# Gated DeltaNet's triangular blocks inverted with 32 and 64 wide tensor engine tiles, in place of 128 wide products and transposes

## The chip, the cores and the metric

The kernel runs on one core of a Trainium2 chip. The time is that of the device from start to end of one execution, in microseconds (us). The engines of a core run in parallel, each in the order of its own instructions: the tensor engine (PE, with its weight loads as PEld), VectorE (DVE), ScalarE (ACT), GpSimd (POOL), and SyncE (SP), which here only issues transfers between HBM and on-chip memory. A transfer is issued by an engine's queue and waits there, with all that is queued behind it, until what it needs is there.

## The reference

Four residual layers, each a token mixer, a cross-attention and a gated MLP; layer 2's mixer is the gated DeltaNet, which alone is touched. It works on 256 tokens, 8 query/key heads and 16 value heads, in chunks. Within a chunk it solves a unit lower triangular system:

```
    decay = jnp.exp(jnp.where(incl, gc[..., :, None] - gc[..., None, :], -jnp.inf))
    kb = k * beta[..., None]
    m = jnp.where(strict, jnp.einsum('bnhlk,bnhsk->bnhls', kb, k) * decay, 0.0)
    a_mat = m + jnp.eye(chunk, dtype=jnp.float32)
    rhs = jnp.concatenate([v * beta[..., None], kb * jnp.exp(gc)[..., None]], axis=-1)
    sol = lax.linalg.triangular_solve(a_mat, rhs, left_side=True, lower=True, unit_diagonal=True)
```

## The kernel before

Weights come from HBM as 128x1024 tiles (`raw`, four buffers, loaded by SP). ScalarE casts each to its high part `wH`, VectorE subtracts to get the low part `wL` (`prep`), and the tensor engine takes three products for each pair of parts (`mm3`, lines 168 to 170). One tile feeds 24 such products of 128x256, called weight products below. In the DeltaNet they go to the PSUM tile `gps` (48 tiles) and then to `acc` (16 tiles of the output projection).

`gdn` works on chunks of 128 tokens. A head of the loop is a query/key head with two value heads and two chunks, so it has four 128x128 triangular matrices, index `a`, kept side by side in a 128x512 tile. `head` is a generator: at each `yield cost, latency` it hands back to a scheduler of the program (`Weave`), which runs the next piece once the projections have issued that many nanoseconds of tensor engine work. So the work of several heads is woven between weight products. The compiler's scheduler then settles the order within each engine. The names in a head, in its order:

- `l2` and `grb`: norms of query and key, and the decays by row; `E` the decays.
- `gp` (line 942): the products of keys with keys and queries. VectorE makes `MT` from it, the transposed triangular matrices with their decays (line 948).
- SP stores `MT` to a scratch in HBM (`gd`, line 956) and loads its 16x16 diagonal blocks back as `blk` (line 957), 32 blocks on 32 partitions.
- GpSimd inverts these blocks by substitution in 30 instructions (`tm`, `ub`, lines 969 and 971) and stores the result to a second scratch, zeroed outside the blocks (line 973).
- SP loads that as `U` (line 987), the inverse so far, transposed.
- The solve. Four transposes give `Tm` from `U` (`tps`). Then blocks of 16 are joined to blocks of 32, and those to 64: with the part of `MT` that a level needs (`ml`, masked by `lvl`), `yps` = ml x Tm, `ups` = U x Y, Tm -= ups, and four transposes write U anew. The last level, 64 to 128, uses 64x64 products and writes U directly.
- Then the right-hand sides: `gvp`, `gsp`, `gs`, `grp`, `gop`, and at the end `gbp`. `S` is the state, copied out of `gs` by ScalarE.

All small products are float32 and run as two passes on the tensor engine, so that four products show as x8 in the rows.

Of the kernel before, what the change touches and what calls it, by code (L numbers as in the profile page):

```python
# [40 lines left out]
CM = {}  # L41
# [45 lines left out]
def tile_trunk(ctx: ExitStack, tc: tile.TileContext, io: dict, out: bass.AP, layers=range(DEPTH), parts="mxf", final=True):  # L87
    nc = tc.nc
    ACT, DVE, POOL, PE = nc.scalar, nc.vector, nc.gpsimd, nc.tensor
# [21 lines left out]
    def mx(name):  # L111
        return ps_mx.tile([P, 512], F32, tag="mx", name=name)
# [4 lines left out]
    def flat(ap):  # L117
        return ap.rearrange("p a b -> p (a b)")
# [19 lines left out]
    cm = cst.tile([P, CM["bd"]], F32, name="cm")  # L138
# [705 lines left out]
    def diag(d):  # L844
        return bass.AP(tensor=d.tensor, offset=d.offset, ap=[[16 * P + 16, 32], [P, 16], [1, 16]])

    def rows(d):
        return d[:, :P, :].rearrange("a s l -> s a l")

    def gdn_scratch():  # L850
        with phase("gz") as z:
            zt = z.tile([P, 4, P], F32, name="zt")
            POOL.memset(zt, 0.0)
            d = [[dr.tile([4, P + 1, P], F32, name=f"gd{i}{j}") for j in range(2)] for i in range(2)]
            for j in range(2):
                nc.sync.dma_start(out=rows(d[1][j]), in_=zt)
        return d

    def gdn(layer, ic, gname):
        with ExitStack() as ex:  # L860
# [4 lines left out]
            gcm = U1([P, 768], "gcm")  # L865
            nc.scalar.dma_start(out=gcm, in_=io["cm"][:, CM["lvl"]:CM["lvl"] + 768])
# [8 lines left out]
            (a, b), (c, d) = [[flat(t[:, :2]), flat(t[:, 2:])] for t in (U1([P, 4, P], "E"), U1([P, 4, P], "Y"))]  # L875
            rw, tcol = U1([P, T], "grw", F32R), U1([P, 2, 64], "gtcol")
            POOL.memset(pk, 0.0)
            with tc.high_priority(offset=EVAC):
# [8 lines left out]
                DVE.tensor_tensor_scan(out=pk[:16], data0=gcm[:16, 512:768], data1=ga, initial=0.0,  # L887
# [13 lines left out]
            lvl = gcm[:, :2 * P].rearrange("p (a b) -> p a b", a=2)  # L901
# [4 lines left out]
            def head(h, qk):  # L906
# [48 lines left out]
                d0, d1 = scr[0][h % 2], scr[1][h % 2]  # L955
# [5 lines left out]
                ml = W(f"ml{h % 2}", 1)  # L961

                def level(l):
                    DVE.tensor_tensor(out=ml, in0=MT, in1=lvl[:, l:l + 1, :].to_broadcast([P, 4, P]), op=ALU.mult)

                POOL.tensor_copy(ub.rearrange("p a b -> p (a b)"), gcm[:32, 256:512])
# [6 lines left out]
                nc.gpsimd.dma_start(out=diag(d1), in_=ub)  # L973
                kd, qd = W2("kd", 3), W2("gqd", 3)
# [19 lines left out]
                Tm = W("Tm")  # L994
                ACT.copy(flat(Tm), tps)
                yield 440, LAT[2]
                for l in range(2):
                    yp = mx("yps")
                    for a in range(4):
                        PE.matmul(yp[:, a * P:(a + 1) * P], ml[:, a, :], Tm[:, a, :], start=a == 0, stop=True,  # L1000
                                  skip_group_check=True)
                    if l == 0:
                        level(1)
                    Y = W("Y", 1)
                    ACT.copy(flat(Y), yp)
                    yield 870, LAT[3]
                    up = mx("ups")
                    for a in range(4):
                        PE.matmul(up[:, a * P:(a + 1) * P], U[:, a, :], Y[:, a, :], start=a == 0, stop=True,
                                  skip_group_check=True)  # L1010
                    DVE.tensor_tensor(out=flat(Tm), in0=flat(Tm), in1=up, op=ALU.subtract)
                    yield 870, LAT[4]
                    tps = mx("tps")
                    for a in range(4):
                        PE.transpose(tps[:, a * P:(a + 1) * P], Tm[:, a, :], ident)
                    ACT.copy(flat(U), tps)
                    yield 440, LAT[14]

                yp = mx("yps")
                for a in range(4):  # L1020
                    PE.matmul(yp[64:, a * 64:(a + 1) * 64], MT[:64, a, 64:], Tm[:64, a, :64], start=a == 0, stop=True,
                              skip_group_check=True)
                Y = W("Y", 1)
                ACT.copy(Y[64:, :, :64], yp[64:, :T].rearrange("p (a b) -> p a b", a=4))
                yield 440, LAT[3]
                up = mx("ups")
                for a in range(4):
                    PE.matmul(up[:64, a * 64:(a + 1) * 64], Y[64:, a, :64], U[64:, a, 64:], start=a == 0, stop=True,
                              skip_group_check=True)
                DVE.tensor_tensor(out=U[:64, :, 64:], in0=U[:64, :, 64:], in1=up[:64, :T].rearrange("p (a b) -> p a b", a=4),  # L1030
                                  op=ALU.subtract)
                yield 440, LAT[13]
# [309 lines left out]
```

## Time and profile before

| | us |
|---|---|
| median of 3 executions | 2039.09 |
| lowest, highest | 2039.07, 2043.4 |
| profiled execution | 2039.35 |
| its span, first to last instruction | 2037.6 |
| tensor engine busy | 1987.2 (98%) |
| VectorE busy | 1575.0 (77%) |
| ScalarE busy | 1280.4 (63%) |
| GpSimd busy | 341.6 (17%) |

Busy is the time in which at least one instruction of the engine is under way. The share is a mean over a program of many stages, and says nothing of which engine a single stage waits for. The DeltaNet mixer lies between about 985 and 1285 us.

### The profile page before, as it was taken

How to read it: one execution, taken by the hardware profiler on the slowest of the kernel's cores; microseconds unless marked ns; L12 is line 12 of the kernel's file. 1: busy time of each engine (PE TensorE's matmuls, PEld its weight loads, DVE VectorE, ACT ScalarE, POOL GpSimd, SP SyncE). 2: the span in 40 equal slices, each digit the busy share in tenths (PEclk: the TensorE clock that was granted, in tenths of full speed). 3: DMA queues.
4: the chain of work that ended last, by engine and by line, in shares of the span. 5: the costliest groups of instructions: out<-in, count | busy, mean ns of one | idle time of the engine just before them, and what ended most of it. 6: DMA issues, size and time to landing. Idle time of an engine off the chain costs nothing.

```text
span 2037.6 us, 42013 instructions
## 1 busy us (share of the span) xinstructions
PE 1987.2 (98%) x17020; PEld 1942.3 (95%) x17020; DVE 1575.0 (77%) x2417; ACT 1280.4 (63%) x1874; POOL 341.6 (17%) x468
## 2 busy tenths in 40 slices
PE   8999999999999999999999999999999999999997
PEld 8999999999999899999998899999999999999997
DVE  6899777875788778866786875878756999777875
ACT  6687666654565566555676875666545778666553
POOL 2032211000133110001064451110001133201001
PEclk9999999999999999999999999999999999999999
DMA  7655545666644546666544333457666565545663
GB/s 242 202 186 173 174 146 167 216 193 181 211 156 135 150 133 211 200 192 192 188 123 136 107 111 123 140 162 217 193 177 200 196 197 171 179 136 176 195 193 121
DMA packets 112770, 351.53 MB, mean 173 GB/s; under 512 B 15744, under 2 KB 25664, under 8 KB 112576
## 3 DMA queue, kind: packets, MB, share of 16 engines
q1 hardware_dynamic: 106176, 333.42, 52.9%
q10 hardware_dynamic: 6144, 15.17, 2.2%
q8 instruction: 133, 2.18, 0.4%
q0 software_dynamic: 256, 0.26, 0.1%
q14 instruction: 61, 0.50, 0.1%
HBM read 344.81 MB, written 4.00 MB: 171 GB/s over the span
## 4 chain that ended last, share of the span: by engine, by line
PE 78%; issue 5%; DVE 5%; ACT 4%; POOL 2%; DMA 1%; DVEq 0%; SPq 0%; POOLq 0%; ACTq 0%
PE ffps L170 8%; PE ffps L169 8%; PE ffps L168 8%; PE acc L168 6%; PE acc L169 6%; PE acc L170 6%; PE mps L168 4%; PE mps L170 3%; PE mps L169 3%; DVE wL L161 2%; PE qps L170 2%; PE qps L168 2%; PE qps L169 2%; PE kvps L168 1%; PE kvps L170 1%
## 5 line engine op out<-in xcount | busy, mean ns | idle before, releaser
L161 DVE TENSOR_TENSOR wL<-raw,wH 128x1024 fp32r<-128x1024 f32 (+2 forms) x639 | 786.3, 1232 | 326.8 <-ACT wH L160 324.3
L160 ACT CAST wH<-raw 128x1024 fp32r<-128x1024 f32 (+2 forms) x639 | 658.9, 1032 | 535.6 <-PE ffps L169 160.8
L168 PE MATMUL ffps<-hH,wH 128*128 128x256 f32 x1376 | 380.6, 277 | 0.0
L169 PE MATMUL ffps<-hL,wH 128*128 128x256 f32 x1376 | 379.8, 276 | 0.0
L170 PE MATMUL ffps<-hH,wL 128*128 128x256 f32 x1376 | 379.2, 276 | 0.0
L168 PE MATMUL acc<-aH,wH 128*128 128x256 f32 x1232 | 344.5, 280 | 0.0
L170 PE MATMUL acc<-aH,wL 128*128 128x256 f32 x1232 | 341.4, 277 | 0.6 <-DVE wL L161 0.6
L169 PE MATMUL acc<-aL,wH 128*128 128x256 f32 x1232 | 341.0, 277 | 0.0
L169 PEld LDWEIGHTS ffps<-hL,wH 128*128 128x128 f32 x1376 | 258.3, 188 | 0.1
L168 PEld LDWEIGHTS ffps<-hH,wH 128*128 128x128 f32 x1376 | 258.3, 188 | 0.1
L170 PEld LDWEIGHTS ffps<-hH,wL 128*128 128x128 f32 x1376 | 258.0, 188 | 0.0
L168 PEld LDWEIGHTS acc<-aH,wH 128*128 128x128 f32 x1232 | 231.5, 188 | 1.3 <-issue 0.7
L170 PEld LDWEIGHTS acc<-aH,wL 128*128 128x128 f32 x1232 | 231.3, 188 | 1.1 <-DVE wL L161 1.0
L169 PEld LDWEIGHTS acc<-aL,wH 128*128 128x128 f32 x1232 | 231.6, 188 | 0.6
L168 PE MATMUL mps<-hH,wH 128*128 128x256 f32 x768 | 218.0, 284 | 0.0
L169 PE MATMUL mps<-hL,wH 128*128 128x256 f32 x768 | 213.8, 278 | 0.0
L170 PE MATMUL mps<-hH,wL 128*128 128x256 f32 x768 | 213.0, 277 | 0.0
L212 POOL TENSOR_TENSOR ns<-nsq 128x256 f32<-128x256 f32 x13 | 10.7, 821 | 856.7 <-ACT nsq L209 856.7
L168 PEld LDWEIGHTS mps<-hH,wH 128*128 128x128 f32 x768 | 144.3, 188 | 2.9 <-issue 2.4
L169 PEld LDWEIGHTS mps<-hL,wH 128*128 128x128 f32 x768 | 144.4, 188 | 0.7
L170 PEld LDWEIGHTS mps<-hH,wL 128*128 128x128 f32 x768 | 144.4, 188 | 0.3
L170 PE MATMUL gps<-hH,wL 128*128 128x256 f32 x448 | 127.6, 285 | 0.6 <-DVE wL L161 0.6
(410 smaller groups left out, 4670.1 us busy)
## 6 DMA issues: line engine op xcount, KB each, us to landing
raw<-f_up SPq DMA_DIRECT2D x176, 512.0 KB, 4.1
raw<-m_in SPq DMA_DIRECT2D x96, 512.0 KB, 3.6
raw<-f_down SPq DMA_DIRECT2D x80, 512.0 KB, 4.2
raw<-xa_kv SPq DMA_DIRECT2D x60, 512.0 KB, 4.3
raw<-g_in SPq DMA_DIRECT2D x48, 512.0 KB, 4.1
raw<-m_out SPq DMA_DIRECT2D x32, 512.0 KB, 3.6
raw<-xa_q SPq DMA_DIRECT2D x32, 512.0 KB, 3.6
raw<-xa_o SPq DMA_DIRECT2D x32, 512.0 KB, 3.6
```

The costliest lines, as they stand in the source:

```text
L160: ACT.copy(H[:, c], raw[:, c])
L161: DVE.tensor_tensor(out=L[:, c], in0=raw[:, c], in1=f32(H[:, c]), op=ALU.subtract)
L168: PE.matmul(dst, aH, bH, start=start, stop=False, skip_group_check=True)
L169: PE.matmul(dst, aH, bL, start=False, stop=False, skip_group_check=True)
L170: PE.matmul(dst, aL, bH, start=False, stop=stop, skip_group_check=True)
L212: self.eng.tensor_tensor(out=self.sum, in0=sq[:, :T], in1=sq[:, T:], op=ALU.add)
```

## The change

The inverse is kept in both forms from the start. GpSimd writes its blocks also transposed (`ut`) to a third scratch, and SP loads from it `Tm`, now only the 64 columns that are used, in two halves. Each level is done on the diagonal tiles alone: level 16 with products on 32x32 tiles (for `up` with 16 columns), level 32 likewise, level 64 with 64x64 tiles. Both `U` and `Tm` are updated from products, with no transposes and no masked copy of `MT`; a per-partition factor `low` (made once from `lvl`) clears the part that level 16 must not take. Since all products of the solve go through one helper, they carry its one line (1000) in the changed kernel. The constants are loaded in two pieces, and two of the softplus scratch tiles take other places.

```diff
-            d = [[dr.tile([4, P + 1, P], F32, name=f"gd{i}{j}") for j in range(2)] for i in range(2)]
+            d = [[dr.tile([4, P + 1, P], F32, name=f"gd{i}{j}") for j in range(2)] for i in range(3)]
             for j in range(2):
-                nc.sync.dma_start(out=rows(d[1][j]), in_=zt)
+                for i in (1, 2):
+                    nc.sync.dma_start(out=rows(d[i][j]), in_=zt)
...
+            DVE.tensor_reduce(out=low, in_=lvl, axis=AX.X, op=ALU.max)
+            DVE.tensor_scalar(out=low, in0=low, scalar1=-1.0, scalar2=1.0, op0=ALU.mult, op1=ALU.add)
...
                 nc.gpsimd.dma_start(out=diag(d1), in_=ub)
+                POOL.tensor_copy(ut, ub.rearrange("p a b -> p b a"))
+                nc.gpsimd.dma_start(out=diag(d2), in_=ut)
...
                 nc.sync.dma_start(out=U, in_=rows(d1))
-                level(0)
+
+                Tm = wk.tile([P, 4, 64], F32, tag="Tm", name="Tm", bufs=2)
+                for b in (0, 64):
+                    nc.sync.dma_start(out=Tm[b:b + 64], in_=d2[:, b:b + 64, b:b + 64].rearrange("a s l -> s a l"))
                 yield 0, LAT[1]
-
-                tps = mx("tps")
+                Q = [slice(32 * i, 32 * i + 32) for i in range(4)]
+                quad = lambda ps, o, w: ps[:, o:o + 4 * w].rearrange("p (a b) -> p a b", a=4)
+
+                def block(d, lhsT, rhs, first):
+                    PE.matmul(d, lhsT, rhs, start=first, stop=True, skip_group_check=True)
+
+                ps = mx("yps")
+                yp = quad(ps, 0, 16)
                 for a in range(4):
-                    PE.transpose(tps[:, a * P:(a + 1) * P], U[:, a, :], ident)
...
+                    for i, q in enumerate(Q):
+                        block(yp[q, a], MT[q, a, q], Tm[q, a, 32 * (i % 2):32 * (i % 2) + 16], a == 0)
+                Y = wk.tile([P, 4, 16], F32, tag="Y0", name="Y0", bufs=1)
+                ACT.activation(out=Y, in_=yp, func=AF.Copy, scale=low)
+                yield 300, 1200
+                ps = mx("ups")
+                tp, up = quad(ps, 0, 16), quad(ps, 64, 16)
                 for a in range(4):
...
+                    for q in Q[:3]:
+                        block(tp[q, a], U[q, a, q], Y[q, a], a == 0)
                 for a in range(4):
...
+                    for i, q in enumerate(Q):
+                        block(up[32 * i:32 * i + 16, a], Y[q, a], U[q, a, 32 * i + 16:32 * i + 32], a == 0 and i == 3)
+                for i in (0, 2, 1):
+                    d = Tm[Q[i], :, 32 * (i % 2):32 * (i % 2) + 16]
+                    DVE.tensor_tensor(out=d, in0=d, in1=tp[Q[i]], op=ALU.subtract)
+                for i in (1, 3, 0, 2):
+                    ACT.activation(out=U[32 * i:32 * i + 16, :, 32 * i + 16:32 * i + 32], in_=up[32 * i:32 * i + 16], func=AF.Copy,
+                                   scale=-1.0)
+                yield 600, 1800
+
+                ps = mx("yps")
+                yp = quad(ps, 0, 32)
+                for a in range(4):
+                    for b in (0, 2):
+                        block(yp[Q[b + 1], a], MT[Q[b], a, Q[b + 1]], Tm[Q[b], a, :32], a == 0)
...
+                yield 300, 1200
+                ps = mx("ups")
+                tp, up = quad(ps, 0, 32), quad(ps, P, 32)
+                for a in range(4):
+                    block(tp[Q[1], a], U[Q[1], a, Q[1]], Y[Q[1], a], a == 0)
+                    for b in (0, 2):
+                        block(up[Q[b], a], Y[Q[b + 1], a], U[Q[b + 1], a, Q[b + 1]], a == 0)
...
+                yield 400, 1500
+
+                ps = mx("yps")
+                yp = quad(ps, 0, 64)
+                for a in range(4):
+                    block(yp[64:, a], MT[:64, a, 64:], Tm[:64, a, :], a == 0)
...
```

The change also alters the order on the engines. On SP, from head 0's `U` on (the scratches are numbered; `gd_12451` and `gd_12452` hold U's blocks, `gd_12453` the transposed ones), before:

```order
L987 DMA U<-gd_12451 128x4x128
L159 DMA raw<-g_in 128x1024
L956 DMA gd_12450<-MT 128x4x128
L957 DMA blk<-gd_12450 32x16x16
L159 DMA raw<-g_in 128x1024 x3
L987 DMA U<-gd_12452 128x4x128
L159 DMA raw<-g_in 128x1024
```

and in the changed kernel:

```order
L990 DMA U<-gd_12451 128x4x128
L994 DMA Tm<-gd_12453 64x4x64
L962 DMA gd_12450<-MT 128x4x128
L994 DMA Tm<-gd_12453 64x4x64
L963 DMA blk<-gd_12450 32x16x16
L159 DMA raw<-g_in 128x1024 x4
L962 DMA gd_12449<-MT 128x4x128
L990 DMA U<-gd_12452 128x4x128
```

Head 1's MT and block loads stand between the halves of Tm and the next weights, and no weight is loaded between U and MT any more. On GpSimd, at the end of head 0's block, before:

```order
L969 TENSOR_TENSOR tm<-ub,blk 32x15
L971 TENSOR_TENSOR ub<-ub,tm 32x15
L973 DMA gd_12451<-ub 32x16x16
L966 COPY ub<-gcm 32x256
L960 TENSOR_TENSOR gatt<-gatt,cm 128x512
```

and in the changed kernel:

```order
L970 TENSOR_TENSOR tm<-ub,blk 32x15
L972 TENSOR_TENSOR ub<-ub,tm 32x15
L974 DMA gd_12451<-ub 32x16x16
L975 COPY ut<-ub 32x256
L976 DMA gd_12453<-ut 32x16x16
L967 COPY ub<-gcm 32x256
L966 TENSOR_TENSOR gatt<-gatt,cm 128x512
```

The copy `ut` and its store have come in behind U's store, ahead of the next head's work. On the tensor engine, where head 7's solve starts (weight products to `acc`), in the changed kernel:

```order
L1118 MATMUL gbp<-ident,on 128x128 x4
L1000 MATMUL yps<-Tm,MT 32x32 x8
L1000 MATMUL yps<-Tm,MT 32x16 x16
L1000 MATMUL ups<-Y_15884,U 32x32
L1000 MATMUL ups<-U,Y_15884 32x32
L168 MATMUL acc_15846<-aH,wH 128x256
L169 MATMUL acc_15846<-aL,wH 128x256
L170 MATMUL acc_15846<-aH,wL 128x256
L1000 MATMUL ups<-Y_15904,U 32x16 x12
L1000 MATMUL ups<-U,Y_15904 16x16 x16
```

Where before a group was four transposes or four 128-wide products, it is now 8 to 28 small ones. Here head 7's first group (32x16, x16) stands 94 weight products behind its `gp`; before, its first transposes stood 193 behind.

## Rows read from the trace of the kernel before

**Rows 1.** The page, busy time of the tensor engine and its weight loads, with share of the span and instructions.

```profile
PE 1987.2 (98%) x17020; PEld 1942.3 (95%) x17020; DVE 1575.0 (77%) x2417; ACT 1280.4 (63%) x1874; POOL 341.6 (17%) x468
```

**Rows 2.** Busy time of each engine from 1015.1 to 1266 us: length, then busy us (instructions) of PE, PEld, DVE, ACT and POOL, granted tensor engine clock, DMA share, GB/s.

```profile
1015.10:1266.00 250.90, 240.58 (x1935) 225.46 (x1936) 183.23 (x357) 182.34 (x276) 112.78 (x262) 0.99 0.38 120
```

**Rows 3.** Timeline of the tensor engine from 1015.1 to 1266 us: start us, us until the last of them ends, what; in brackets the idle time before it and what ended it. The heads: `gp` at 1015.13 is head 0, 1101.31 head 3, 1133.31 head 4; `tps` at 1127.35 is head 3, 1161.33 head 4, 1244.40 head 7; `grp` is head 0; `gbp` head 6.

```profile
1015.13 0.70 PE L942 MATMUL gp<-kq 128*128 128x256 f32 x2 [0.64 <-DVE kq L919]
...
1073.11 0.80 PE L1064 MATMUL grp<-S,kd 128*128 128x128 f32 x2 [3.21 <-ACT S L1059]
...
1101.31 1.03 PE L942 MATMUL gp<-kq 128*128 128x256 f32 x4
...
1127.35 0.60 PE L993 MATMUL tps<-ident,U 128*128 128x128 f32 x4
...
1133.31 1.03 PE L942 MATMUL gp<-kq 128*128 128x256 f32 x4
...
1161.33 0.66 PE L993 MATMUL tps<-ident,U 128*128 128x128 f32 x4 [1.23 <-DMA U<-gd]
...
1244.40 0.60 PE L993 MATMUL tps<-ident,U 128*128 128x128 f32 x4
...
1265.95 0.60 PE L1091 MATMUL gbp<-ident,on 128*128 128x128 f32 x4
```

**Rows 4.** Waits of the SP queue between 980 and 1290 us: who waits, for what: us in total, times, longest us.

```profile
SPq L987 <- DMA gd<-ub: 86.2, 8, 16.9
```

**Rows 5.** Timeline of the SP queue: start us, us, issue. The first four are around U of head 0, then U of head 1 with the weight behind it, then U of heads 3, 6 and 7.

```profile
1041.11 0.38 SPq L987 DMA_DIRECT2D U<-gd  x1
1041.58 0.46 SPq L159 DMA_DIRECT2D raw<-g_in  x1
1042.09 0.42 SPq L956 DMA_DIRECT2D gd<-MT  x1
1047.63 0.33 SPq L957 DMA_DIRECT2D blk<-gd  x1
...
1066.36 0.38 SPq L987 DMA_DIRECT2D U<-gd  x1
1066.84 0.45 SPq L159 DMA_DIRECT2D raw<-g_in  x1
...
1123.00 0.38 SPq L987 DMA_DIRECT2D U<-gd  x1
...
1219.64 0.37 SPq L987 DMA_DIRECT2D U<-gd  x1
...
1234.78 0.38 SPq L987 DMA_DIRECT2D U<-gd  x1
```

**Rows 6.** Timeline of the tensor engine in heads 0 and 2 (columns as in rows 3). `gps` is a weight product, `tps` transposes, `yps` at 1048.74 the 128-wide products, at 1060.65 the 64-wide ones.

```profile
1044.74 0.60 PE L993 MATMUL tps<-ident,U 128*128 128x128 f32 x4
...
1045.30 0.28 PE L170 MATMUL gps<-hH,wL 128*128 128x256 f32 x1
...
1047.42 0.28 PE L170 MATMUL gps<-hH,wL 128*128 128x256 f32 x1
...
1048.74 1.06 PE L1000 MATMUL yps<-Tm,ml 128*128 128x128 f32 x8
...
1049.76 0.28 PE L169 MATMUL gps<-hL,wH 128*128 128x256 f32 x1
...
1060.12 0.60 PE L1015 MATMUL tps<-ident,Tm 128*128 128x128 f32 x4
1060.65 0.68 PE L1021 MATMUL yps<-Tm,MT 64*64 64x64 f32 x8
...
1061.48 0.28 PE L169 MATMUL gps<-hL,wH 128*128 128x256 f32 x1
```

**Rows 7.** Timeline of the tensor engine in the HGRN2 mixer of layer 1, a group with 32-column outputs between weight products.

```profile
586.97 0.28 PE L170 MATMUL ips<-wH,hL 128*128 128x256 f32 x1
587.18 0.64 PE L759 MATMUL op<-S,qd 128*32 128x128 f32 x14
...
587.97 0.28 PE L169 MATMUL ips<-wL,hH 128*128 128x256 f32 x1
```

**Rows 8.** Timeline of GpSimd in head 2: first of the block, two in between, the store, and the copy behind it; the DVE row is the cast that runs at the same time.

```profile
1074.17 0.20 POOL L969 TENSOR_TENSOR tm<-ub,blk 32x15 f32<-32x15 f32 x1 [6.14 <-DMA blk<-gd]
...
1077.42 0.29 POOL L969 TENSOR_TENSOR tm<-ub,blk 32x60 f32<-32x60 f32 x1
1077.78 1.16 POOL L971 TENSOR_TENSOR ub<-ub,tm 32x60 f32<-32x60 f32 x1
...
1086.45 0.68 POOL L973 DMA_DIRECT2D gd<-ub  x1 [0.30 <-POOL ub L971]
1088.62 0.39 POOL L966 COPY ub<-gcm 32x256 f32<-32x256 f32 x1 [1.49 <-DMA gd<-ub]
...
1077.46 1.33 DVE L161 TENSOR_TENSOR wL<-raw,wH 128x1024 fp32r<-128x1024 f32 x1 [2.27 <-ACT wH L160]
```

**Rows 9.** DMA issues: what, queue, number, size of one, median us from issue to landing.

```profile
gd<-MT SPq DMA_DIRECT2D x8, 256.0 KB, 2.5
U<-gd SPq DMA_DIRECT2D x8, 256.0 KB, 2.8
```

**Rows 10.** The instructions that write the masked copy `ml`: line, engine, operation, number: ns least/median/most, first and last start, shapes.

```profile
L964 DVE TENSOR_TENSOR ml<-MT,gcm x16: 676/686/701, 1025.5 to 1247.0; 128x512 f32<-128x512 f32 x16
```

More of the change, by code (lines that the diff above doesn't have):

```diff
@@ L864, in gdn @@
             oT = U1([P, 16, T], "goT")
-            gcm = U1([P, 768], "gcm")
-            nc.scalar.dma_start(out=gcm, in_=io["cm"][:, CM["lvl"]:CM["lvl"] + 768])
+            gcm = U1([P, 512], "gcm")
+            nc.scalar.dma_start(out=gcm, in_=io["cm"][:, CM["i16"]:CM["i16"] + 512])
+            lvl, low = U1([P, P], "glvl"), U1([P, 1], "glow")
+            nc.scalar.dma_start(out=lvl, in_=io["cm"][:, CM["lvl"]:CM["lvl"] + P])
+            DVE.tensor_reduce(out=low, in_=lvl, axis=AX.X, op=ALU.max)
+            DVE.tensor_scalar(out=low, in0=low, scalar1=-1.0, scalar2=1.0, op0=ALU.mult, op1=ALU.add)
             baps = bank("baps")
@@ L874, in gdn @@
             be = flat(be)[32:48]
-            (a, b), (c, d) = [[flat(t[:, :2]), flat(t[:, 2:])] for t in (U1([P, 4, P], "E"), U1([P, 4, P], "Y"))]
+            (a, b), (c, d) = [[t[:, 0, :], t[:, 1, :]] for t in (flat(U1([P, 4, P], "E")).rearrange("p (a b) -> p a b", a=2), U1([P, 2, T], "gsq"))]
             rw, tcol = U1([P, T], "grw", F32R), U1([P, 2, 64], "gtcol")
@@ L885, in gdn @@
                 DVE.tensor_scalar(out=ga, in0=ga, scalar1=na, scalar2=None, op0=ALU.mult)
-                DVE.tensor_tensor_scan(out=pk[:16], data0=gcm[:16, 512:768], data1=ga, initial=0.0,
+                DVE.tensor_tensor_scan(out=pk[:16], data0=gcm[:16, 256:512], data1=ga, initial=0.0,
                                        op0=ALU.mult, op1=ALU.add)
@@ L900, in gdn @@
             cols = weave.push(late(12000, columns()))
-            lvl = gcm[:, :2 * P].rearrange("p (a b) -> p a b", a=2)
             W = lambda nm, b=2: wk.tile([P, 4, P], F32, tag=nm, name=nm, bufs=b)
@@ L954, in head @@
                 tm = wk.tile([32, 16, 16], F32, tag="tm", name="tm", bufs=1)
-                d0, d1 = scr[0][h % 2], scr[1][h % 2]
+                ut = wk.tile([32, 16, 16], F32, tag="ut", name="ut", bufs=1)
+                d0, d1, d2 = [s[h % 2] for s in scr]
                 nc.sync.dma_start(out=rows(d0), in_=MT)
@@ L960, in head @@
                 POOL.tensor_tensor(out=att, in0=att, in1=tri.unsqueeze(1).to_broadcast([P, 4, P]), op=ALU.mult)
[L961 to L966, printed above, removed]
+                POOL.tensor_copy(ub.rearrange("p a b -> p (a b)"), gcm[:32, :256])
                 for j in range(15):
@@ L995, in head @@
[L995 to L1017, printed above, removed]
@@ new lines, in head @@
+                for i in (1, 3, 0, 2):
[7 more added lines that the diff above has]
+                        block(yp[Q[b + 1], a], MT[Q[b], a, Q[b + 1]], Tm[Q[b], a, :32], a == 0)
+                Y = wk.tile([P, 4, 32], F32, tag="Y1", name="Y1", bufs=1)
@@ new lines, in head @@
+                ACT.copy(Y[Q[1]], yp[Q[1]])
+                DVE.tensor_copy(Y[Q[3]], yp[Q[3]])
+                yield 300, 1200
[5 more added lines that the diff above has]
+                        block(up[Q[b], a], Y[Q[b + 1], a], U[Q[b + 1], a, Q[b + 1]], a == 0)
+                DVE.tensor_scalar(out=Tm[Q[1], :, :32], in0=tp[Q[1]], scalar1=-1.0, scalar2=None, op0=ALU.mult)
@@ new lines, in head @@
+                for b in (2, 0):
+                    ACT.activation(out=U[Q[b], :, Q[b + 1]], in_=up[Q[b]], func=AF.Copy, scale=-1.0)
+                yield 400, 1500
[3 more added lines that the diff above has]
+                    block(yp[64:, a], MT[:64, a, 64:], Tm[:64, a, :], a == 0)
+                Y = wk.tile([P, 4, 64], F32, tag="Y", name="Y", bufs=1)
+                ACT.copy(Y[64:], yp[64:])
+                yield 480, 1200
@@ L1034, in head @@
+                ps = mx("ups")
+                up = quad(ps, 0, 64)
+                for a in range(4):
+                    block(up[:64, a], Y[64:, a, :], U[64:, a, 64:], a == 0)
+                DVE.tensor_scalar(out=U[:64, :, 64:], in0=up[:64], scalar1=-1.0, scalar2=None, op0=ALU.mult)
+                yield 480, LAT[13]
                 while h not in vz or (h and h - 1 not in done):
```

13 lines of the change are left out of this document (removed).

## The prediction

> **What bounds the kernel now.** I read the page first: the tensor engine is busy 98% of the span [rows 1], so only its work or its waits can move the end. Then I asked for the stretch that the change touches, from head 0's first `gp` product (1015.13) to head 6's `gbp` (1265.95): 250.9 us, in which the tensor engine is busy 240.6 and idle 10.3 [rows 2, 3]. The rest of the span is the same in both kernels.
>
> Then I looked for what ends the idle time, and found a chain beside the tensor engine. Each head's products give MT; SP stores it and loads its 16x16 blocks back; GpSimd inverts them in 30 small instructions (`tm`, `ub`); GpSimd stores the result, and SP loads U. SP runs in order and also loads the weights, so weight loads behind a waiting U wait too: SP spends 86.2 us before the eight U loads, up to 16.9 at once [rows 4]. Two of the tensor engine's waits end with it: 1.23 us for U itself in head 4, and 3.21 us at 1073.11 in head 0 [rows 3], where, in ScalarE's order, the copy of S stands behind the cast of the weight that SP issued only at 1066.84, right behind U [rows 5]. Elsewhere the tensor engine has enough other work between a head's `gp` and its first product on U: in heads 3 and 7 that product starts without a wait [rows 3].
>
> **The tensor engine's own work.** Prices from one stretch [rows 6]: a weight product 0.118 us (18 steps from 1045.30 to 1047.42); four transposes 0.44 (1044.74 to 1045.30, less one product); four 128-wide float32 products, two passes each, 0.90 (1048.74 to 1049.76, less one); four 64-wide ones 0.80 (1060.12 to 1061.48, less the transposes and one weight product). A head's solve is now 3 x 0.44 + 4 x 0.90 + 2 x 0.80 = 6.5 us.
>
> The new solve has no transposes, 64 products on 32x32 tiles (128 passes) and the two 64-wide groups. Nothing in the trace is that small. The nearest row is the other mixer's group of 14 passes with 32-column outputs: 586.97 to 587.97 is 1.00 us, less two weight products 0.76 [rows 7]. One after the other at the 128-wide price (0.90 / 8 = 0.11 each) they would take 1.6, so passes on different column tiles do run side by side: four rounds of 0.11 explain 0.44, and the 0.33 left is the cost of changing the array's shape and back. The 64-wide group then has 0.47 for 8 passes, 0.058 each. A small pass costs at most those 0.058 (7.4 us a head, all in a row); with half the columns and two to four tiles at once it is 0.007 to 0.015. I take the latter, nearest to the row with the same tile width: 1.3 us a head. With six changes of shape (2.0) and 0.94 for the 64-wide passes a solve is 4.3 us, 2.2 less. Counting every group in both orders at these prices, the same stretch has 241.8 us of work before (the trace says 240.6 busy, so the count holds) and 17.3 us less after, five groups split by weight products included.
>
> The Trainium skill speaks against the small products: "TensorEngine Tiling (Array Packing)", section Instruction Overhead, gives each matmul some 60 cycles however few its columns, and advises against tiling a dimension that is already small. By it, estimated at the granted clock (0.99 of 2.4 GHz in this stretch [rows 2]), 128 passes would cost 3.2 us a head instead of 1.3, and the gain would be 2 us instead of 17.3. The row of 14 passes agrees that passes overlap but does not show so few columns.
>
> **What is added to the chain.** Behind U's store GpSimd now copies the transposed blocks (0.39, as its copy at 1088.62) and issues a second store (0.68, as at 1086.45) [rows 8]; SP issues U, waits for that store, and issues Tm in two loads. The first product needs Tm. Bounds: 0.5 if the stores overlap fully, 2 if copy and store each meet a VectorE cast; I take 1.1. Behind the waiting Tm loads stand the next MT store or block load and then the weights.
>
> VectorE and ScalarE lose more than they gain (two masks, two 128x512 subtractions and five 128x512 copies a head go, small operations come); they end no wait above except through casts, so this counts nothing. Two more zero stores and the split constant load at the mixer's start go out while four weights are loaded ahead; without that cover they cost the two issues, under 1 us. The scratch tiles of the softplus change place; I take the time of the first `gp` as even, within 1.5 us.
>
> **Where the saving goes.** The chain does not get shorter, but the work that covers it does, and the new order puts a head's first product closer to its `gp`: 98 weight products apart in head 3 (112 before), 97 in head 4 (107), 111 in head 6 (173), 94 in head 7 (193). Work at the prices above against the chain:
> - Head 3: from `gp` (1101.31) to U landed was 24.5 us (issued 1123.00, lands in 2.8) [rows 3, 5, 9]. Plus 1.1 is 25.6, against 18.9 of work: wait 6.7.
> - Head 4: 28.0 (1133.31 to 1161.33). Between that and 24.5 I take 26, plus 1.1, against 22.3: wait 4.8.
> - Heads 6 and 7: GpSimd does both in a row; U7 followed U6 by 15.1 (1219.64, 1234.78). 26 + 1.1 + 15.1 = 42.2, against 31.8: wait 10.4.
> - Head 0: `gp` to U landed 28.8 (1041.11 + 2.8); plus 1.1, and 0.9 for two issues between the halves of Tm: 30.8, against 27.0: wait 3.8.
> - Heads 0 and 1 at the first S: U landed to the resumption was 29.2. Tm1 adds 1.1, but MT1's store (5.5 us, 1042.09 to 1047.63, behind a weight) no longer has a weight ahead of it and may land in the usual 2.5 [rows 9]. I take 27.8, against 22.3: wait 5.5.
>
> Sum 31.2 in place of 10.3. So 2039.35 (span 2037.6, 1.75 around it) - 17.3 - 10.3 + 31.2 = 2043, or 0.3 less against the median of 2039.09. What a measurement of this kernel can tell from no change is about 0.2%, 4.1 us; this is at its edge.
>
> **Rivals.**
> 1. *The chain shortens by itself (ends faster).* GpSimd's small instructions take 0.29 us, but 1.16 when they meet VectorE's cast: `ub` at 1077.78 ran 1.16 while the cast ran 1077.46 to 1078.79 [rows 8]. Fewer VectorE operations and a waiting tensor engine mean fewer such meetings. Head 2's block, with two such meetings, took 12.3 us to its store (1074.17 to 1086.45). Head 4's chain of 28.0 against head 3's 24.5 leaves room for some four more. If the heads that I put above 24.5 came down to it, the waits would shrink by some 10: 2033. It decides from 1.3 us a chain on (six of them pass 4 + 3.6). For it: the mask operation, 16 times 0.69 us, goes [rows 10]. Against: the 48 casts of this mixer, which hold GpSimd most, all stay. The Trainium skill, "SBUF — State Buffer", section SBUF: two separate sides, has GpSimd locked out for the whole of a VectorE operation with two SBUF inputs; the pair of rows agrees.
> 2. *The waits don't come:* the saving is kept whole, with waits as before: 2039.35 - 17.3 = 2022. Against it stands the fixed chain of 24.5 and more in every head.
> 3. *Small passes one after the other,* 0.058 each: 6.1 us more a head, 49 in all, of which the waits hide some 20: 2072. By the price on the Trainium skill's page "TensorEngine Tiling (Array Packing)", Instruction Overhead, the estimate is 2050.
>
> **Chances and range.** Waits take the place of work, 2036 to 2052: 0.62, of which 0.36 above 2043.2 and 0.26 within 4.1 us. Rival 1, 2026 to 2037: 0.22 (0.18 faster, 0.04 same). Rival 2: 0.06. Rival 3: 0.07. Anything else, 0.03, counted as same. Faster 0.24, same 0.33, slower 0.43. Six chains at 1.5 us each are 9 us if all err alike; the range 2028 to 2053 holds the first case, most of rival 1 and the cheap end of rival 3. The first case alone: 2036 to 2052.
>
> **What would show it.** Right: tensor engine work about 17 us less in the stretch (solve products 16 at a time in 0.6 us, changes of shape of about 0.33), and waits of 4 to 7 us before the first small product of heads 0, 3, 4, 6 and 7 that end with the landing of Tm, U or a weight; SP waiting over 86 us at U and Tm. Wrong: no wait above 2 us at those places; GpSimd blocks near 10 us; or solve groups of several us.

## The result and the profile after

The changed kernel takes 2064.31 us (median of 4 executions, 2063.74 to 2067.99): 1.0109 of the kernel before, interval 1.0076 to 1.0142. It is slower by about 1%; 2043 was forecast, with 2053 as the upper end. The page of the profiled execution, busy time as in [rows 1]:

```profile
PE 1989.1 (96%) x17692; PEld 1937.5 (94%) x17692; DVE 1566.3 (76%) x2427; ACT 1284.4 (62%) x1906; POOL 348.7 (17%) x484
```

The tensor engine is busy as long as before, in a span 23.9 us longer, although it has less to do. The whole DeltaNet from the first `gp` to the first product of the next mixer, columns as in [rows 2], before:

```profile
1015.13:1287.48 272.35, 261.94 (x2119) 246.62 (x2119) 199.06 (x379) 195.10 (x297) 115.25 (x265) 0.99 0.38 121
```

and in the changed kernel:

```profile
1017.29:1311.21 293.92, 261.07 (x2768) 238.72 (x2769) 189.62 (x385) 196.97 (x326) 123.25 (x281) 0.90 0.39 115
```

21.6 of the 23.9 us are in this stretch, and 2.2 before its first `gp`. Length less busy is idle: 10.4 before, 32.9 after. The granted clock is 0.99 and 0.90, and the records of the clock know two levels only, 1.00 (2.4 GHz) and 0.50 (1.2 GHz): 6.8 us at half clock before, 61.4 after. Half of that, where the engine was not idle anyway, is counted as lost: 3.1 and 27.0 us. What is left is counted as work at full clock: 258.9 and 234.0. So **work -24.8, idle +22.5, half clock +23.9**, together 21.6.

Two things in this split are not what they seem. A weight product starts every 0.118 us at 1.00 [rows 6] and every 0.213 at 0.50 (rows below), so of its time about 45% is lost and not half: by that pace 21.3 of half clock and -22.2 of work. And the first `gp`, where the stretch begins, has moved: 268 of the 1152 weight products to `gps` now stand ahead of it, 246 before. These 22, some 2.5 us, left the stretch and lie in the 2.2 ahead of it; they are no work saved. Weight products ahead of `gp` (length, then busy us and number of PE, PEld, DVE and ACT, clock, DMA share, GB/s), before and changed:

```profile
980.00:1015.13 35.13, 29.08 (x246) 28.28 (x246) 5.54 (x12) 2.47 (x5) 1.00 0.61 193
```

```profile
980.00:1017.29 37.29, 31.46 (x268) 30.81 (x268) 6.06 (x14) 2.93 (x7) 1.00 0.67 209
```

The waits of the tensor engine in the changed kernel, columns as in [rows 3]:

```profile
1049.17 0.29 PE L1000 MATMUL yps<-Tm,MT 32*32 32x16 f32 x4 [4.82 <-DMA Tm<-gd]
1050.57 0.61 PE L1000 MATMUL yps<-Tm,MT 32*32 32x16 f32 x28 [1.11 <-DMA Tm<-gd]
...
1094.44 0.24 PE L1000 MATMUL yps<-Tm,MT 32*32 32x16 f32 x4 [3.45 <-DMA Tm<-gd]
...
1128.70 0.35 PE L168 MATMUL gps<-hH,wH 128*128 128x256 f32 x1 [3.73 <-ACT gc L327]
...
1176.47 0.24 PE L1000 MATMUL yps<-Tm,MT 32*32 32x16 f32 x4 [1.28 <-DMA Tm<-gd]
...
1223.98 0.21 PE L1000 MATMUL ups<-Y,U 32*32 32x32 f32 x1 [3.08 <-ACT Y L1033]
...
1243.00 0.43 PE L1000 MATMUL yps<-Tm,MT 32*32 32x16 f32 x28 [1.38 <-DMA Tm<-gd]
...
1251.72 0.63 PE L1118 MATMUL gbp<-ident,on 128*128 128x128 f32 x4 [1.67 <-DVE on L838]
...
1256.82 0.29 PE L1000 MATMUL yps<-Tm,MT 32*32 32x16 f32 x4 [4.10 <-DMA Tm<-gd]
```

Heads 0, 2, 4, 6 and 7 wait for Tm; the waits of 3.73 and 3.08 us end with ScalarE. What follows such a wait is seen in slices of 2 us around head 2's (columns as in [rows 2]):

```profile
1093.00:1095.00 2.00, 0.24 (x4) 0.14 (x4) 0.00 (x0) 0.00 (x0) 0.00 (x0) 1.00 0.56 90
1095.00:1097.00 2.00, 1.86 (x57) 1.60 (x58) 1.29 (x3) 0.73 (x3) 0.00 (x0) 0.75 0.82 293
1097.00:1099.00 2.00, 2.00 (x23) 1.66 (x24) 1.00 (x2) 1.35 (x3) 0.00 (x0) 0.50 1.02 416
...
1107.00:1109.00 2.00, 2.00 (x11) 2.00 (x11) 0.00 (x0) 1.84 (x4) 0.00 (x0) 0.50 0.00 0
1109.00:1111.00 2.00, 2.00 (x32) 1.65 (x31) 0.48 (x2) 0.19 (x1) 0.00 (x0) 0.84 0.00 0
```

From 1097 on the engine is busy throughout, at 0.50. The kernel before has the same thing once, around its 3.21 us wait [rows 3]:

```profile
1071.00:1073.00 2.00, 0.00 (x0) 0.00 (x0) 0.55 (x1) 1.63 (x3) 0.00 (x0) 0.87 0.08 22
1073.00:1075.00 2.00, 1.89 (x9) 1.89 (x10) 1.70 (x4) 0.06 (x1) 0.64 (x3) 0.50 0.82 172
...
1079.00:1081.00 2.00, 1.92 (x16) 1.90 (x16) 1.42 (x5) 0.86 (x2) 1.59 (x6) 0.92 0.35 135
```

The price of a small group at full clock (head 1, 56 passes between weight products; columns as in [rows 3]), and weight products at half clock, nine steps of 0.213 us:

```profile
1085.35 0.28 PE L168 MATMUL gps<-hH,wH 128*128 128x256 f32 x1
1085.56 0.40 PE L1000 MATMUL ups<-Y,U 32*32 32x16 f32 x21
...
1085.83 0.41 PE L1000 MATMUL ups<-U,Y 32*16 32x16 f32 x31
1086.16 0.38 PE L169 MATMUL gps<-hL,wH 128*128 128x256 f32 x1
1086.39 0.28 PE L170 MATMUL gps<-hH,wL 128*128 128x256 f32 x1
...
1107.19 0.41 PE L168 MATMUL gps<-hH,wH 128*128 128x256 f32 x1
...
1109.11 0.41 PE L168 MATMUL gps<-hH,wH 128*128 128x256 f32 x1
```

From the product ahead of the group to the second one behind it are 1.04 us. Less two weight products, as the prediction counted in [rows 7], the 56 passes and the change of the array's shape cost 0.80.

### The profile page after: what moved, and what is told of

It reads as the page before. It is cut to its first block, busy times and chain, and to the rows that moved or that the text cites. A ratio compares the mean times of both kernels' runs of the same rounds, so it can differ in the third digit from the quotient of the medians.

```text
span 2061.5 us, 43436 instructions
## 1 busy us (share of the span) xinstructions
PE 1989.1 (96%) x17692; PEld 1937.5 (94%) x17692; DVE 1566.3 (76%) x2427; ACT 1284.4 (62%) x1906; POOL 348.7 (17%) x484
## 4 chain that ended last, share of the span: by engine, by line
PE 75%; issue 6%; POOL 5%; DVE 5%; ACT 3%; DMA 2%; SPq 0%; DVEq 0%; POOLq 0%; ACTq 0%
PE ffps L170 8%; PE ffps L168 8%; PE ffps L169 8%; PE acc L168 6%; PE acc L169 6%; PE acc L170 6%; PE mps L168 3%; PE mps L170 3%; PE mps L169 3%; POOL ub L972 2%; DVE wL L161 2%; PE qps L170 2%; PE qps L169 2%; PE qps L168 2%; POOL tm L970 1%
## 5 line engine op out<-in xcount | busy, mean ns | idle before, releaser
L212 POOL TENSOR_TENSOR ns<-nsq 128x256 f32<-128x256 f32 x13 | 10.7, 821 | 861.4 <-ACT nsq L209 861.4
L168 PE MATMUL gps<-hH,wH 128*128 128x256 f32 x448 | 131.6, 294 | 3.7 <-ACT gc L327 3.7
```

The costliest lines, as they stand in the source:

```text
L168: PE.matmul(dst, aH, bH, start=start, stop=False, skip_group_check=True)
L212: self.eng.tensor_tensor(out=self.sum, in0=sq[:, :T], in1=sq[:, T:], op=ALU.add)
```

## The experiments

Executions on other chips and at other times differ by some 10 us outside the DeltaNet (last section), so the table compares the stretch, split as above (half clock as half) from one profiled execution of each kernel; the ratio is that of whole times, with its interval. "Chain" is the mean over the heads from a head's first `gp` to the issue of Tm's load (of its second half where there are two), or of U's where Tm is not loaded. Some expectations count the stretch or its parts otherwise (e5 and e7 297 for 293.9, e6 275.4 for 272.4); comparisons here go by the table. The 22 weight products that left the stretch stand ahead of it in the changed kernel and all that is built on it (24 in e3), but not in e12, e13 and e15: across that line a stretch compares 2.5 us too short.

| kernel | stretch | idle | half clock | work | chain | ratio |
|---|---|---|---|---|---|---|
| before | 272.4 | 10.4 | 3.1 | 258.9 | 29.0 | |
| changed | 293.9 | 32.9 | 27.0 | 234.0 | 31.0 | 1.011 (1.008-1.014) |
| e7 changed again | 292.0 | 32.7 | 25.0 | 234.3 | 31.0 | 1.010 (1.007-1.014) |
| e1 waits filled | 294.6 | 22.7 | 25.6 | 246.2 | 31.2 | 1.015 (1.011-1.018) |
| e2 Tm transposed | 272.8 | 21.9 | 8.0 | 242.9 | 28.3 | 1.001 (0.999-1.004) |
| e3 before, Tm loaded | 285.8 | 26.6 | 5.7 | 253.4 | 31.2 | 1.008 (1.004-1.011) |
| e4 changed, short chain | 266.9 | 20.6 | 11.6 | 234.6 | 23.2 | 0.999 (0.996-1.001) |
| e5 changed, GpSimd's queue | 311.7 | 46.0 | 32.9 | 232.9 | 34.5 | 1.021 (1.017-1.025) |
| e6 e2, GpSimd's queue | 289.3 | 33.1 | 13.5 | 242.7 | 32.1 | 1.014 (1.009-1.019) |
| e9 Tm first | 289.0 | 34.3 | 20.3 | 234.4 | 30.3 | 1.009 (1.006-1.012) |
| e10 e2, load later | 294.4 | 29.7 | 23.8 | 240.9 | 30.3 | 1.013 (1.006-1.019) |
| e11 e2, solve later | 291.3 | 30.9 | 19.5 | 240.9 | 30.1 | 1.010 (1.005-1.015) |
| e12 before, load later | 291.6 | 25.2 | 6.9 | 259.4 | 29.9 | 1.010 (1.006-1.013) |
| e13 small solve alone | 281.3 | 23.0 | 13.8 | 244.4 | 27.7 | 1.005 (1.002-1.008) |
| e14 changed, old places | 285.7 | 33.4 | 17.6 | 234.7 | 31.7 | 1.007 (1.004-1.011) |
| e15 before, short chain | 273.0 | 11.6 | 1.7 | 259.7 | 18.7 | 1.000 (0.997-1.002) |

### What brings the clock down: e1 and e8

**e1**, ahead of the first small product:

```diff
                 ps = mx("yps")
+                for i in range({0: 44, 2: 34, 7: 40}.get(h, 0)):
+                    PE.matmul(ps[:, :T], hH[:, i % 8, :P], hL[:, i % 8, :], start=True, stop=True, skip_group_check=True)
                 yp = quad(ps, 0, 16)
```

> The changed kernel with idle work put into three of its waits: ahead of the first small product of heads 0, 2 and 7 the tensor engine does 44, 34 and 40 more weight-sized products (128x256) whose results are overwritten. In the changed kernel these heads wait 4.8 + 1.1, 3.4 + 0.5 and 4.1 + 0.4 us there, and each wait is followed by a stretch at a granted clock of 0.50 (from 1048, 1096 and 1253 us, together 37.5 us). The fillers are 118 x 0.118 = 13.9 us of work in place of 14.3 us of idle time. Theory A (a wait of the tensor engine costs a second time, since the clock falls to half behind it and all products then take twice as long): the three half-clock stretches are gone, some 15 us of loss with them, time 2047 to 2053. Theory B (the small products themselves bring the clock down, whatever the engine did before them): half clock stays at the three places, time 2062 to 2067. Theory C (the waits cost only their own length, the records of the clock matter little): the same time as B, and no change of the pace of the products.

The filler took 12.2 us of work, idle fell by 10.2, and the loss to half clock stayed (25.6). Theory A's 15 us did not come, and theory C falls with the pace of 0.213 us at 0.50. The filler also changed the order, so this is no clean fill: other waits came, 6.08 us at most. But the clock also fell at 1086.9, 1162.0, 1182.5 and 1261.0 behind waits of only 1.0 to 2.3 us, and at 1271.2 with hardly any (columns as in [rows 2]):

```profile
1264.40:1271.20 6.80, 6.62 (x168) 5.88 (x167) 0.93 (x4) 2.74 (x9) 0.00 (x0) 1.00 0.57 182
1271.20:1273.20 2.00, 2.00 (x23) 1.60 (x16) 0.71 (x2) 0.26 (x1) 0.00 (x0) 0.50 0.00 0
```

Of the 168 products ahead of that fall 138 are small, and the engine waits 0.18 us. Counted over the runs: with the old solve (before, e3, e12, e15) 17 waits of 1.0 to 1.7 us left the clock at 1.00. With the small products (changed, e1, e4, e7, e9) it fell in nine places with no wait over 1.35 in the 7 us ahead, this one among them; ten other waits of 1.0 to 1.7 us left it at 1.00 there too. So small products can bring it down with a short wait or none, but not every time.

**e8** leaves waits out and puts small products between weight products that have no waits:

```diff
+    def probe(kind):
+        ps = mx("pr")
+        if kind == 1:
+            for a in range(14):
+                for i in range(4):
+                    q = slice(32 * i, 32 * i + 32)
+                    PE.matmul(ps[q, 16 * a:16 * a + 16], ident[q, q], ident[q, 32 * i:32 * i + 16], start=a == 0, stop=True,
...
+        if kind == 2:
+            for a in range(5):
+                PE.matmul(ps[:, :T], hH[:, a, :P], hL[:, a, :], start=True, stop=True, skip_group_check=True)
...
```

> A measurement of the clock alone, on the kernel before: in the gated MLPs, where the tensor engine has weight products without waits, products are added whose results nobody reads. Layer 0: a group of 56 small products (32x16 tiles, 112 passes) after every 12 weight products, from unit 4 to unit 15; layer 1: the same after every 6; layers 2 and 3, at the same places: 5 more weight-sized products (128x256), after every 12 and every 6. Theory A (only waits bring the clock down): full clock in all four layers; a small group costs about 0.7 us as in the changed kernel. Theory B (small products bring it down even without a wait): half clock in layers 0 and 1, or in 1 alone, full clock in 2 and 3.

The four places in its one execution, in the order of the layers, columns as in [rows 2]:

```profile
352.00:531.00 179.00, 143.50 (x5920) 131.09 (x5920) 58.98 (x85) 41.79 (x60) 0.00 (x0) 0.92 0.27 83
904.00:1230.00 326.00, 312.45 (x11073) 284.47 (x11076) 56.74 (x80) 40.73 (x59) 0.00 (x0) 0.50 0.15 46
1763.00:1858.00 95.00, 95.00 (x805) 95.00 (x804) 57.64 (x84) 40.36 (x59) 0.00 (x0) 1.00 0.47 146
2295.00:2420.00 125.00, 125.00 (x1055) 125.00 (x1054) 55.95 (x77) 38.34 (x52) 0.00 (x0) 1.00 0.35 106
```

In layer 1, with a small group after every 6 weight products, the tensor engine is busy 312 of 326 us and runs at 0.50 all the while; it is back at 1.00 at 1233, 2 us behind the last group. With 128-wide products at the same places the clock stays at 1.00. So theory B holds for dense small products: a tensor engine that does them can be busy and stay at half clock. It is not quite without waits, since the small groups make their own (last section): the first fall came with one of 1.94 us at 903.5. In layer 0 such waits are 36 us of 179, the clock is at 0.50 for only 27 us, and nothing is decided there.

The Trainium skill, "TensorE: Matmul & The Clock Gate", section "HAM oscillation — how this bites in real kernels", tells of a kernel whose waits for transfers bring it to the half clock again and again. These traces agree for the waits of 4.82 and 3.45 us for Tm above; at that of 4.10 the clock fell 0.3 us into the wait, at 1253.0, behind one of 1.67.

### The chain at an unchanged order: e4, e5, e9, e7

In e5, e7 and e9 the tensor engine's order is word for word that of the changed kernel. In e4 it is so up to head 2, and within a few products up to head 5; the expectation's six heads are not quite right. **e4** and **e5**:

```diff
-                for j in range(15):
+                for j in range(7):
```

```diff
-                nc.sync.dma_start(out=rows(d0), in_=MT)
-                nc.sync.dma_start(out=blk, in_=diag(d0))
+                nc.gpsimd.dma_start(out=rows(d0), in_=MT)
+                nc.gpsimd.dma_start(out=blk, in_=diag(d0))
```

> The changed kernel with GpSimd's substitution cut to its first 7 of 15 steps (the last eight steps of the inverse of the 16x16 blocks are left out, so the outputs differ), which makes the chain some 5 to 6 us shorter in each head and leaves the tensor engine's order the same for the first six heads. Theory A (the chain sets the waits, and the waits set the clock): nearly all waits ahead of the first small products go, the half-clock stretches go too, time falls by 30 to 45 us to 2020 to 2034. Theory B (small products bring the clock down by themselves): idle falls by some 20 us but half-clock stretches stay, time 2042 to 2050.

> The changed kernel with two transfers of each head moved to another queue: MT's store and the load of its blocks are issued by GpSimd, which waits for these blocks anyway, and no longer by SP, where MT of head 1 stood 11 us (1036.5 to 1047.4) behind the waiting loads of U and Tm, and where weights stood behind waiting MT stores for 43.6 us in total. The tensor engine's order is word for word that of the changed kernel. Theory A (the waits come in good part from SP's order: what stands behind a waiting U or Tm is late): the stretch from the first gp to the next mixer (297.0 us in the changed kernel) falls by 8 to 20 us. Theory B (the chain through GpSimd sets the waits, whoever issues its transfers): it stays within 4 us, or rises by up to 6 since GpSimd needs some 0.7 us for each issue.

e4: the chain is 7.8 us shorter and the stretch 27.0, idle 12.3 and half clock 15.4 less. That lies between theory A's 30 to 45 and the 14 to 22 that B's times mean: most of the loss to half clock goes with the waits, but 24 us at half clock remain. e5 goes the other way and against both theories: the block loads take 4.0 us on GpSimd's queue instead of 2.5, the chain is 3.5 us longer, and the stretch 17.8, idle 13.1 and half clock 5.9 more. So nothing is won by taking these transfers off SP in this way. In the changed kernel a microsecond of chain in every head comes with 3 to 5 us of the stretch (3.5 by e4, 5.1 by e5).

**e9**, and the loads of U and Tm on SP in the same way:

```diff
-                nc.gpsimd.dma_start(out=diag(d1), in_=ub)
                 POOL.tensor_copy(ut, ub.rearrange("p a b -> p b a"))
                 nc.gpsimd.dma_start(out=diag(d2), in_=ut)
+                nc.gpsimd.dma_start(out=diag(d1), in_=ub)
```

> The changed kernel with the two stores and loads in the other order: GpSimd copies and stores the transposed blocks first and U's behind them, and SP loads Tm first and then U. The first product needs Tm alone, and U only one product later, so the chain to the first product loses about 1.3 us a head; nothing is removed, and the tensor engine's order is word for word that of the changed kernel (stretch 293.9 us, on another chip 292.0). Theory A (the length of the chain to the first product sets the waits and, with them, the clock): idle 31 falls to about 22 and the loss to half clock from 26 to about 18, the stretch to 274 to 284. Theory B (it is SP's time, blocked until the later of the two stores is there, that costs): the stretch stays within 4 us of 293.

Down 4.9 (3.0 against e7), to the edge of theory B and 5 us short of theory A: the first wait is 4.27 us instead of 4.82 and 1.11, but head 7's 5.81 instead of 4.10. Half clock gives 6.7, idle nothing.

> The changed kernel again, beside the others on the same chip, so that the stretch of the DeltaNet can be compared within one chip. Expected from its first profile: 297 us from the first gp product to the next mixer, of which 237.7 work at full clock, 32.1 idle, 27.1 lost to half clock outside the idle time; within 4 us of each if the split is a property of the kernel, farther off if it is chance.

On another chip the split is within 2 us of the first one.

### The parts of the change alone: e2, e3, e13

**e2** (in the changed kernel) and **e3** (in the kernel before, the other way round):

```diff
-                for b in (0, 64):
-                    nc.sync.dma_start(out=Tm[b:b + 64], in_=d2[:, b:b + 64, b:b + 64].rearrange("a s l -> s a l"))
...
+                for a in range(4):
+                    PE.transpose(tps[:, a * P:(a + 1) * P], U[:, a, :], ident)
```

```diff
+                POOL.tensor_copy(blk, ub.rearrange("p a b -> p b a"))
+                nc.gpsimd.dma_start(out=diag(d2), in_=blk)
...
+                Tm = W("Tm")
+                nc.sync.dma_start(out=Tm, in_=rows(d2))
```

> The changed kernel without its longer chain: Tm comes from four tensor engine transposes of U as before (diagonal 64-column halves copied out), so the transposed copy on GpSimd, its store and the two Tm loads are gone; the small products stay. That is 8 x 0.44 = 3.5 us more tensor engine work. Theory A (chain longer by some 1 to 3 us a head, waits, half clock behind them): idle time in the stretch falls from 32 to about 20 us, half-clock stretches from 61 to about 35 us, time about 2042. Theory B (the added store and loads hardly count; the waits come from the shorter solve that covers less): idle and half clock as in the changed kernel, time about 2067.

> The kernel before with one part of the change alone: GpSimd also stores its blocks transposed, and Tm is loaded by one transfer in place of the first four transposes of each head; the rest of the solve (128-wide products, transposes, masks) as before. Tensor engine work 3.5 us less. Theory A (the longer chain costs by itself): idle time grows from 10 to about 20 us and half-clock stretches appear behind waits over 3 us, time 2045 to 2055. Theory B (the old, longer solve covers the added store and loads): idle as before, time 2035 to 2037.

Both theory A; e2's ratio of 1.001 is that of its 2042. It gives back the whole loss and no more: against the kernel before, 16.0 us of work less, 2.5 of them only moved out of the stretch, stand beside 11.5 more idle and 4.9 more half clock. e3, with the old solve, loses only 2.6 more to half clock, but idle is up 16.2.

**e13** puts the small solve into the kernel before. Against the solve of e2, which it takes over:

```diff
-                yield 300, 1200
+                yield 870, LAT[3]
...
-                yield 600, 1800
+                yield 870, LAT[4]
+                yield 440, LAT[14]
```

> The kernel before with the solve alone replaced: Tm from four transposes of U, then the small products as in the changed kernel; no second store, no loads of Tm, and the costs and latencies at which the solve hands back to the weave are those of before, so that the written order of all else stays. Work expected as in the transposed variant, 245 us. Theory A (the clock falls only behind waits, and waits come only from the order and the chain): idle about 12, half clock about 4, stretch 258 to 264, a kernel faster than before by 0.4 to 0.7%. Theory B (small products bring the clock down, and less cover makes waits, even at the old places): idle 18 to 25, half clock 8 to 20, stretch 270 to 285.

Theory B. 14.5 us of work are saved, and idle takes 12.6 and half clock 10.7. Its longest wait shows how. It is at the product on S of head 0 (columns as in [rows 3]):

```profile
1073.65 1.22 PE L1092 MATMUL grp<-S,kd 128*128 128x128 f32 x4 [6.08 <-ACT S L1087]
```

On SP, columns as in [rows 5], U of head 1 and the weight behind it:

```profile
1066.60 0.38 SPq L984 DMA_DIRECT2D U<-gd  x1
1067.08 0.45 SPq L159 DMA_DIRECT2D raw<-g_in  x1
```

U and its weight go out at the same time as before (1066.36 and 1066.84, [rows 5]) and S is there at the same time (1073.11, [rows 3]); the engine has only come there sooner, and waits 6.08 us instead of 3.21.

### Other orders: e6, e10, e11, e12, e14, e15

**e12** changes two numbers of the kernel before, **e10** the same two in e2's kernel, and **e11** only the first of them in e2's kernel (23500, 5620).

```diff
-    LAT = [21000, 5620, 1450, ...
+    LAT = [23500, 3120, 1450, ...
```

> The kernel before with nothing changed but the two first entries that set the weave (21000 and 5620 made 23500 and 3120: U's load 2.5 us later in the written order, its use at the same place). The same move on the changed kernel with transposes raised its stretch from 272.8 to 294.4 us. Theory A (each move of the written order costs, since the other entries fit this one order of the kernel before): the stretch rises from 272.4 by 8 us or more also here, with idle 18 or more. Theory B (the old solve, longer on the tensor engine and without small products, stands the move): the stretch stays within 5 us of 272.4, half clock under 5 us.

> The changed kernel with Tm from four transposes, and the U load put 2.5 us later in the written order (first two entries that set the weave, 21000 and 5620, made 23500 and 3120), so that fewer weights stand behind a U that still waits on SP. With the transposes alone the stretch took 272.8 us, 19.6 of it idle. Theory A (two of its waits, 4.7 us at the product on S and 4.0 us at the first transposes, come from SP's order): idle about 12, stretch 260 to 266, faster than before by 0.3 to 0.7%. Theory B (what is gained there is lost at other places, since each move changes the whole order): 270 to 278.

> As the run before, but with the solve also 2.5 us of weight work later (23500 and 5620): more cover between a head's gp and its first product, and heads that finish later. Theory A: idle about 10, half clock about 4, stretch 258 to 266. Theory B: the last two heads end later behind the last weights, 272 to 282.

Theory A for e12; e10 and e11 lie above even their theory B. Each of these moves costs 18 to 22 us, in the kernel before too (19.2). That one's order is one at which waits are few, 10.4 us; every other kernel here but e15 has 20 or more. At 20 to 27 us of idle time the two solves differ in the clock: 5.7 and 6.9 us lost with the old one (e3, e12), 8.0 to 25.6 with the new one (e2, e4, e13, e1).

**e14** is the changed kernel with the old numbers at the solve's yields, **e6** is e2 with e5's queue, and **e15** is the kernel before with e4's cut.

> The changed kernel whole, but with the costs and latencies at which the solve hands back to the weave as before (870, 440 and the old latencies for 300 to 600 and 1200 to 1800). The order is another one again: for instance head 7's first product stands 115 instead of 94 weight products behind its gp. Theory A (the change's own costs and latencies put the solve at worse places): idle 20 or less, stretch under 280. Theory B (any new order costs, and the chain with Tm's store and loads is the longer one anyway): idle 25 to 33, half clock 15 to 27, stretch 285 to 298.

> The changed kernel with Tm from four transposes (no second store, no Tm loads) and with MT's store and block load issued by GpSimd. With the transposes alone the stretch took 272.8 us: 245.2 of work, 19.6 idle, 8.0 lost to half clock; two of its waits (4.7 us at the product on S of head 0, and the late MT of head 1, made at 1044.9 and stored at 1054.0) stand behind a waiting U on SP. Theory A: idle falls to about 12 and half clock to about 4, the stretch to 260 to 266, which is 10 to 15 less than the kernel before's 275.4, and the whole is faster than before by 0.4 to 0.8%. Theory B (GpSimd's own issue and waits eat it): 270 to 276, same as before.

> The kernel before with GpSimd's substitution cut to 7 of 15 steps (the last eight steps are left out, so the outputs differ), as was done to the changed kernel, which fell from 293.9 to 266.9 us. Theory A (the old solve covers its chain, 9 us idle, so a shorter chain has little to give): the stretch falls by no more than 8 us, to 264 to 272. Theory B (the chain sets the pace before as well): it falls by 15 us or more.

e14 is theory B, at its low end: 8.2 us less than the changed kernel, all of it half clock. e6 missed both theories: 16.5 us more than e2, with 3.8 more of chain. e15 is theory A in its sense: 10.3 us less of chain bring nothing, the stretch does not even fall (273.0). The old solve in its order covers its chain; the new one does not.

None of these kernels is measurably faster than the one before.

## Why the prediction was wrong

- **The clock: the step that failed.** The sum priced every product at full clock. The stretch's 0.99 was read as "full", and the half clock around the 3.21 us wait is not in the prediction. Half clock costs 23.9 us more than before by the table, 21.3 by the pace of the weight products. With the other errors below, 2043 + 21.3 (half clock) - 2.4 (work) + 1.6 (idle) is 2063.5.
- **Work.** Forecast -17.3, and the table has -24.8. Of these 2.5 are the 22 weight products that left the stretch, and 2.6 come from counting half clock as half, by the pace of the weight products. So about 19.7 were saved, and the term was sized well. So were its prices. Small passes do run side by side, and the 56 above cost 0.80 with the change of shape, where 56 at 0.010 and 0.33 make 0.89. Rival 3 falls with that: 56 passes at 0.058 would be 3.2 us. So does the price from the Trainium skill's page "TensorEngine Tiling (Array Packing)", section Instruction Overhead, by which they would take 1.4 us, an estimate; the measured row decides.
- **Waits in place of work, the main case.** Idle of 31.2 was forecast and 32.9 measured, but not at the places named. Heads 0 and 4 wait 5.9 and 1.6 (3.8 and 4.8 forecast), heads 6 and 7 together 5.9 (10.4), head 3 not at all (6.7), the first S not at all (5.5); head 2 (3.9), a weight product (3.73) and a product on Y (3.08) do. That the sum fits is in part chance.
- **The longer chain.** Forecast 1.1 us; the mean to the last load's issue rose by 2.0. SP waited for the store of U and that of Tm 78.7 us, not more than 86.2 [rows 4], but 43.6 for MT instead of 24.4:

```profile
SPq L990 <- DMA gd<-ub: 68.8, 8, 15.2
SPq L962 <- DVE MT L953: 43.6, 6, 13.8
SPq L994 <- DMA gd<-ut: 9.9, 8, 2.8
```

- **Rival 1** (GpSimd's blocks get faster): hardly; from a block's first instruction to its store it takes 14.0 us on average and took 14.2, and from `gp` 26.3 and 26.8. **Rival 2** (no waits): no, as its own argument said.
- **First `gp`:** even within 1.5 us was taken; it starts 2.2 later, since 22 more weight products stand ahead of it, which the stretch no longer holds. The sum loses nothing by it.

What stays open: how the 22.5 us of idle divide between the longer chain and the mere loss of the old order. e3 and e2 speak for the chain (16.2 more, and 11.0 less), e12 shows as much from order alone, and each of the three changes the order. What is shown is that the small solve alone, without the longer chain and at the old written places, turns most of its saving into waits (e13), and that it lowers the clock where the old one does not.

## What to carry to other kernels

Work taken from an engine that waits for a chain beside it can turn into waits, even if that engine is busy 98% of the time; ask first what covers the chain. Behind a wait read the granted clock in slices of a few microseconds, not the mean of the stage, and expect dense small tiles to keep it low. Where an order was fitted to a kernel by numbers, change it and the work apart: a move of 2.5 us alone cost 1%.

## What the runs showed of the hardware

Dense small products held the clock at 0.50 for 326 us while the engine was busy 96% of them (e8, layer 1). The clock also fell to 0.50 behind 6.8 us in which the engine was busy 6.62 and 138 of 168 products were small (e1).

In a long run of small products the tensor engine sits idle at times with nothing in the profile that it waits for ("issue"; e8, layer 0, columns as in [rows 3]); why is not shown:

```profile
380.36 0.71 PE L244 MATMUL pr<-ident 32*32 32x16 f32 x62
381.64 0.60 PE L244 MATMUL pr<-ident 32*32 32x16 f32 x50 [0.57 <-issue]
...
383.75 0.74 PE L244 MATMUL pr<-ident 32*32 32x16 f32 x66
385.65 0.57 PE L244 MATMUL pr<-ident 32*32 32x16 f32 x46 [1.15 <-issue]
```

Weight products come in two paces at full granted clock. In a gated MLP that no kernel here touches, the same 100 us hold 885 products in the profiled execution of the kernel before and 851 in that of e2:

```profile
800.00:900.00 100.00, 100.00 (x885) 100.00 (x884) 78.50 (x111) 58.34 (x81) 0.00 (x0) 1.00 0.67 206
```

```profile
800.00:900.00 100.00, 100.00 (x851) 100.00 (x850) 77.04 (x108) 55.52 (x79) 0.00 (x0) 1.00 0.64 199
```

That is 113 and 118 ns each. The slower pace lasted for a whole MLP (755 to 980 us in e2), 9 us of it, in some executions and not in others; what sets it is open.
